# Weight sums and quarters on VectorE, TensorE's order written down from the layers' turn on, and another order of the seven products

## The chip, the cores and the metric

The kernel runs on one core of one Trainium2 chip. The metric is the device time of one execution in microseconds (us), as the median of several runs. Five engines work beside each other, each through its own instruction queue in order: TensorE (PE; its weight loads are shown as PEld), VectorE (DVE), ScalarE (ACT), GpSimd (POOL) and SyncE (SP), which here mostly issues DMA transfers.

## The reference

Two residual layers over 1024 tokens of width 1024. Each normalises its input by rows, scales and shifts it with vectors that come from a condition `c`, mixes tokens, and projects back.

```python
for layer in range(DEPTH):
    mod = jnp.einsum("bd,de->be", cond, ada_w[layer]) + ada_b[layer]
    shift, scale, gate = jnp.split(mod, 3, axis=-1)
    h = rms_norm(x, pre_gain[layer]) * (1.0 + scale[:, None, :]) + shift[:, None, :]
    if layer % N_MIXERS == 0:
        y = diff_attention(h, ...)      # 8 heads, softmax over 1024 keys
    else:
        y = retention(h, w_in, w_out)   # 4 heads, chunkwise state
    x = x + gate[:, None, :] * rms_norm(y, post_gain[layer])
...
# retention: q, k, v, g = split(h @ w_in); per chunk: scores, state, outputs
out = head_rms_norm(inner_out + cross)
y = silu(g) * out
return y @ w_out
```

## The kernel before

Every f32 matrix is split into two f16 parts, so that a product takes three matmuls for each 128x128 block of weights: high by high, high by low, low by high.

**Layer 0** (attention) ends with the output projection. `out0(t)` multiplies the rows of tile t (48 matmuls, L566), and `residual` and `row_rsqrt` turn them into the next layer's normalised rows `x`: an ACT square with a sum (L578), a DVE product (L579), three small POOL operations on 128x1 (L580, L581 and the power in `rsqrt`, L144), a DVE update `xres` (L583), an ACT square again (L295), two POOL operations (L296, L144), and a DVE scaling (L621).

**The turn.** `out0_hT(j)` takes the rows of tiles 2j and 2j+1, transposes them on PE with the identity matrix (16 transposes, L643) into the two PSUM banks `ps_sc`, lets ACT scale and shift each out of there (L645), and forms sums and differences of the four quarters (`hq`, L651 to L653; on POOL for j of 0 to 2, on DVE for j = 3), each then split into f16 parts (L660 on ACT, L661 on DVE). The list `order` says in which order tiles, transposes and projections are written, "... h0 o4 y6 h1 o5 y7 o6 h2 o7 h3"; a scheduler then sets each engine's real order.

**Layer 1** (retention) multiplies by its input weights in Strassen-Winograd form: seven products of quarter blocks in place of eight. `Columns` holds one unit of weights, 512 columns of queries and keys, of values, or of gates; there are 12 units, three for each of the four heads. `Columns.prepare` loads the quarters `B11`, `B21`, `B12`, `B22` as 128x1024 f32 tiles, forms the sums `T1` to `T4` by four additions on POOL (L779), and splits each into f16 parts (`w`, L792 on ACT, L793 on DVE). Three products are prepared ahead. `Quarters.product(n)` runs product n of `PRODUCTS` (24 matmuls at 256 columns or 12 at 512, L819) for two halves m. Products of one chain letter (`x`, `y`, `z`) accumulate in one PSUM bank; between them ACT copies the bank's state to `held` or `sg` (L827), or DVE combines it with a copy (L833). Chain `y` and later `z` of the second half sit in the single bank `ps_tr`.

The gate columns of a head run with its chunk work between the products: `scores` (L967 on PE, read out by DVE L974), `state` (L991 on PE, L999 and L1002 on DVE), `outputs` (L1014 and L1021 on PE, ACT square L295, the two POOL operations of `row_rsqrt`, DVE L1027). After span 3, `ada_gate` computes a piece of the gate vector (DVE L171 and L173, PE L245, DVE L246 and L247).

**Output products.** For each row tile t the loop at L1134 multiplies by `wo1` (L1142, 36 matmuls for heads 0 to 2 and 12 for head 3, in two column halves n). The weights are loaded by SP (L1106) and split by ACT and DVE (L1110, L1111); the rows come by transposing DMAs (L1126, L1128, L1130), which SP issues too.

Of the kernel before, what the change touches and what calls it, by code (L numbers as in the profile page):

```python
# [87 lines left out]
def trunk(ctx: ExitStack, tc: tile.TileContext, a: dict, out: bass.AP):  # L88
# [143 lines left out]
    def ada_gate(l, j):  # L232
# [11 lines left out]
        ps = tr()  # L244
        nc.tensor.matmul(ps[:, 0:256], ones, acc, start=True, stop=True)  # L245
        nc.vector.tensor_tensor(out=bias, in0=ps[:, 0:256], in1=bias, op=ALU.add)  # L246
        nc.vector.scalar_tensor_tensor(out=gps[l][:, sl], in0=bias, scalar=1.0 / SOUT, in1=gps[l][:, sl], op0=ALU.mult, op1=ALU.mult)  # L247
# [886 lines left out]
    for t in range(NT):  # L1134
        if t + 1 < NT:
            out1_yT(t + 1)
# [43 lines left out]
```

## Time and profile before

| | us |
|---|---|
| median of 3 runs (lowest to highest) | 1421.53 (1421.28 to 1422.03) |
| the profiled execution's own time | 1421.59 |
| its span, first to last instruction | 1419.7 |
| PE busy | 1301.3 (92%) |
| DVE busy | 918.2 (65%) |
| ACT busy | 665.5 (47%) |
| POOL busy | 283.5 (20%) |

The span is what the trace covers; the execution's own time holds 1.9 us more around it. Busy time is a sum over the whole span, so that an engine at 92% can still be waiting in a few places. [...] The idle time in brackets in a timeline is what the engine stood still just before an instruction, with the instruction that ended it.

### The profile page before, as it was taken

What the parts mean: (1) busy time and instruction counts of PE and PEld (TensorE: products, weight loads), DVE (VectorE), ACT (ScalarE), POOL (GpSimd) and SP (SyncE); (2) the same over time, 40 slices, a digit from 0 to 9 for tenths busy, and PEclk for the clock granted to TensorE, in tenths of its full rate; (3) what the DMA queues carried; (4) which work ended last, traced back from release to release, by engine and by line L of the source; (5) the groups of instructions that cost most, each with busy time, mean ns of one, the idle gap of its engine ahead of it and who ended that gap; (6) DMA issues with size and microseconds to landing.
All of it is one profiled execution on the core that took longest, in us unless ns stands there. A gap on an engine that the chain in (4) does not pass through costs nothing.

```text
span 1419.7 us, 21306 instructions
## 1 busy us (share of the span) xinstructions
PE 1301.3 (92%) x8285; PEld 778.7 (55%) x8285; DVE 918.2 (65%) x1722; ACT 665.5 (47%) x1262; POOL 283.5 (20%) x342
## 2 busy tenths in 40 slices
PE   4999999899999997877898999989998999979998
PEld 2445455445455444446786568755865486624443
DVE  5866987996986786765566755766585648841011
ACT  5855545553654664745353545444454535620000
POOL 2000110110111221671234122322222221100000
PEclk9999999999999999998999999999999999999999
DMA  9813564655542566423311251224221543473430
GB/s 298 251 57 76 125 136 122 137 110 126 132 98 47 141 163 107 132 89 86 83 52 60 82 150 55 67 72 132 74 75 37 153 112 119 112 177 70 101 90 30
DMA packets 249174, 153.94 MB, mean 108 GB/s; under 512 B 147576, under 2 KB 237872, under 8 KB 249072
## 3 DMA queue, kind: packets, MB, share of 16 engines
q1 hardware_dynamic: 245904, 141.29, 38.6%
q0 software_dynamic: 3168, 11.28, 2.6%
q8 instruction: 65, 1.06, 0.3%
q14 instruction: 37, 0.30, 0.1%
HBM read 102.21 MB, written 14.68 MB: 82 GB/s over the span
## 4 chain that ended last, share of the span: by engine, by line
PE 33%; DVE 9%; issue 3%; DMA 3%; ACT 3%; POOL 3%; SPq 1%; POOLq 0%; DVEq 0%; ACTq 0%
PE ps_mm L819 15%; PE ps_mm L1142 11%; PE ps_tr L819 4%; DVE w L793 2%; POOL raw L779 2%; DMA raw<-in_ada_w 2%; PE ps_av L1014 1%; DVE y L938 1%; DVE acc L173 1%; DVE sg L833 1%; DVE vr L929 1%; DMA raw<-in_ret_w_in 1%; ACT w L792 1%; PE ps_sc L991 1%; PE ps_av L1021 1%
## 5 line engine op out<-in xcount | busy, mean ns | idle before, releaser
L793 DVE SCALAR_TENSOR_TENSOR w<-raw,w 128x1024 f16<-128x1024 f32 x82 | 118.1, 1440 | 97.8 <-ACT w L792 97.8
L335 PE MATMUL ps_mm<-w,hT 128*128 128x512 f16 x768 | 175.7, 379 | 0.0
L779 POOL TENSOR_TENSOR raw<-raw,raw 128x1024 f32<-128x1024 f32 x48 | 122.4, 2549 | 207.2 <-DVE w L793 189.9
L819 PEld LDWEIGHTS <-hS 128*128 128x128 f16 x1536 | 150.0, 98 | 21.3 <-issue 1.1
L323 PE MATMUL ps_mm<-hT,w 128*128 128x512 f16 x624 | 142.2, 379 | 0.0
L819 PE MATMUL ps_mm<-w,hS 128*128 128x256 f16 x1152 | 132.1, 273 | 0.0
L515 ACT ACTIVATE sb<-sb,mx 128x128 f32<-128x128 f32 (+7 forms) x128 | 98.2, 768 | 63.5 <-DVE mx L508 62.9
L335 PEld LDWEIGHTS <-hT 128*128 128x128 f16 x768 | 74.3, 98 | 82.4
L819 PEld LDWEIGHTS <-w 128*128 128x128 f16 x744 | 75.2, 101 | 74.0 <-issue 9.3
L792 ACT ACTIVATE w<-raw 128x1024 f16<-128x1024 f32 x82 | 86.0, 1048 | 40.7 <-POOL raw L779 15.3
L1142 PE MATMUL ps_mm<-wo,yT 128*128 128x512 f16 x480 | 104.1, 379 | 0.0
L323 PEld LDWEIGHTS <-w 128*128 128x128 f16 x624 | 60.2, 98 | 67.4
L508 DVE CUSTOM_DVE_ANT_0 sb<-ps_sc,table 128x512 f32<-128x512 f32 (+3 forms) x128 | 73.5, 587 | 35.6 <-PE ps_sc L505 27.1
L579 DVE TENSOR_TENSOR po<-ps_mm,gp 128x512 f32<-128x512 f32 x16 | 11.1, 692 | 127.9 <-ACT junk L578 127.9
L566 PE MATMUL ps_mm<-w_o,yT 128*128 128x512 f16 x384 | 93.2, 387 | 0.0
L578 ACT ACTIVATE junk<-ps_mm 128x512 f16<-128x512 f32 x32 | 19.0, 593 | 147.8 <-PE ps_mm L1142 141.1
L819 PE MATMUL ps_mm<-w,hA 128*128 128x256 f16 x768 | 87.9, 273 | 0.0
L819 PEld LDWEIGHTS <-hA 128*128 128x128 f16 x768 | 74.8, 98 | 9.7
L1142 PEld LDWEIGHTS <-yT 128*128 128x128 f16 x480 | 47.0, 98 | 56.6
L173 DVE SCALAR_TENSOR_TENSOR acc<-raw,cond,acc 128x256 f32<-128x256 f32 x140 | 70.9, 517 | 7.1 <-DMA raw<-in_ada_w 5.6
L1142 PE MATMUL ps_mm<-wo,held 128*128 128x512 f16 x288 | 65.3, 388 | 10.3 <-ACT wo L1110 6.3
L819 PE MATMUL ps_mm<-hS,w 128*128 128x512 f16 (+1 forms) x312 | 62.7, 362 | 8.9 <-ACT held L827 8.9
(203 smaller groups left out, 2314.4 us busy)
## 6 DMA issues: line engine op xcount, KB each, us to landing
raw<-in_ret_w_in SPq DMA_DIRECT2D x60, 512.0 KB, 3.6
raw<-in_ada_w SPq DMA_DIRECT2D x40, 512.0 KB, 6.6
raw<-in_da_w_in SPq DMA_DIRECT2D x16, 1024.0 KB, 5.8
raw1o<-in_ret_w_out SPq DMA_DIRECT2D x16, 512.0 KB, 4.7
y_d<-y SPq DMA_DIRECT2D x6, 1024.0 KB, 4.8
x<-in_x SPq DMA_DIRECT2D x8, 512.0 KB, 7.6
raw<-in_ada_w SPq DMA_DIRECT2D x4, 1024.0 KB, 5.2
raw_o<-in_da_w_out SPq DMA_DIRECT2D x4, 1024.0 KB, 5.0
```

Of the source, the lines that this page charges most:

```text
L173: nc.vector.scalar_tensor_tensor(out=acc, in0=parts[k], scalar=cond[:, k : k + 1], in1=acc, op0=ALU.mult, op1=ALU.add)
L323: nc.tensor.matmul(ps, w[:, k, wi, lo : lo + P], hT[k][g][:, xi, :], start=(k == 0 and wi == 0 and xi == 0), stop=(k == NK - 1 and wi == 1),)
L335: nc.tensor.matmul(ps, hT[k][g][:, xi, j * P : (j + 1) * P], w[:, k, wi, :], start=(k == 0 and wi == 0 and xi == 0), stop=(k == NK - 1 and ...
L508: nc.vector.tensor_tensor_reduce(out=sb[:, c, k], in0=ps[c][:, 0:n], in1=table[:, S - L + lo : S - L + lo + n], scale=-es, scalar=(3.0e38 ...
L515: nc.scalar.activation(out=sb[:, c, 0:L], in_=sb[:, c, 0:L], func=AF.Exp, scale=-1.0, bias=mx[:, m0 + c : m0 + c + 1], accum_out=z[:, 4 * ...
L566: nc.tensor.matmul(ps, yT(yi, k), wo[k // 4][:, k % 4, wi, n * 512 : (n + 1) * 512], start=(k == 0 and yi == 0 and wi == 0), stop=(k == NK ...
L578: nc.scalar.activation(out=junk[:, 0:512], in_=src[n], func=AF.Square, accum_out=ss[:, n : n + 1])
L779: add = lambda o, x: nc.gpsimd.tensor_tensor(out=r[o], in0=r[o], in1=r[x], op=ALU.add)
L792: nc.scalar.activation(out=w[:, :, 0, :], in_=r[name], func=AF.Copy, scale=SW)
L793: nc.vector.scalar_tensor_tensor(out=w[:, :, 1, :], in0=r[name], scalar=SW, in1=w[:, :, 0, :], op0=ALU.mult, op1=ALU.subtract)
L819: nc.tensor.matmul(ps[:, pc], l, r, start=(first and i == 0 and k == 0 and wi == 0 and xi == 0), stop=(k == 3 and wi == 1), skip_group_che ...
L1142: nc.tensor.matmul(ps[n], yT1[t][2 * (k // 8) + yi][:, k % 8, :], wo1[k // 4, n][:, k % 4, wi, :], start=(k == 0 and yi == 0 and wi == 0), ...
```

## The change

- The sums of weights in `prepare` and all sums of quarters in `out0_hT` go to DVE.
- From step `o6` on, TensorE's order is the written one; the scheduler no longer orders that engine. The step `h3` leaves the list and stands inside the first unit, behind product 2 of its first half of tokens.
- The fourth of the seven products is now `("z", "S1", "T1")`; before it was the sixth. The reload of `B22` moves to the step of `T4`.
- `ada_gate` returns its second half (matmul and two DVE operations). In layer 1 its sums are written two spans earlier, and the second half stands behind the last span.
- `gated` works on one tile of 512 columns at a time in each head, where heads 0 to 2 took 2048 at once.
- The output products of tiles 0 and 1 run heads 0 to 2 of the first column half for both tiles, then of the second half, then head 3; the second half's sums sit in the bank pair `ps_av`.
- `rsqrt` takes the second addend itself, so that `residual` has two POOL operations in place of three, and scales go into the ACT square.
- Some tiles (`y`, `sg`, `vr`, `y1`) move to the other side of SBUF, and the four `kN` tiles become one.

```diff
@@ rsqrt, residual @@
+    def rsqrt(ss, eps, other=None):
+        r = small.tile([P, 2], F32, name="rs", bufs=6)
+        if other is None:
+            nc.gpsimd.tensor_scalar(out=r[:, 1:2], in0=ss, scalar1=eps, scalar2=None, op0=ALU.add)
+        else:
+            nc.gpsimd.tensor_scalar(out=r[:, 1:2], in0=ss, scalar1=other, scalar2=eps, op0=ALU.add, op1=ALU.add)
+        nc.gpsimd.tensor_tensor(out=r[:, 0:1], in0=r[:, 1:2], in1=negh[:, 0:1], op=ALU.pow)
+        return r[:, 0:1]
...
-        nc.gpsimd.tensor_tensor(out=ss[:, 0:1], in0=ss[:, 0:1], in1=ss[:, 1:2], op=ALU.add)
-        nc.gpsimd.tensor_scalar(out=ss[:, 3:4], in0=ss[:, 0:1], scalar1=1.0 / (D * SOUT**2), scalar2=NORM_EPS, op0=ALU.mult, op1=ALU.add)
-        r = rsqrt(ss[:, 3:4], 1)
+        r = rsqrt(ss[:, 0:1], NORM_EPS, ss[:, 1:2])
@@ out0_hT @@
-            eng = nc.vector if j == 3 else nc.gpsimd
             for i in range(2):
-                eng.tensor_tensor(out=t2[:, i], in0=t[:, 1], in1=t[:, 3 * i], op=ALU.subtract)
+                nc.vector.tensor_tensor(out=t2[:, i], in0=t[:, 1], in1=t[:, 3 * i], op=ALU.subtract)
...
@@ order @@
-        "o1 b5 a6 a7 b6 y4 o2 b7 f0 y5 o3 h0 o4 y6 h1 o5 y7 o6 h2 o7 h3"
+        "o1 b5 a6 a7 b6 y4 o2 b7 f0 y5 o3 h0 o4 y6 h1 o5 y7 o6 h2 o7"
     )
     for c in order.split():
+        if c == "o6":
+            ctx.enter_context(tc.manual_schedule(engines={mybir.EngineType.PE}))
@@ layer 1 @@
     PRODUCTS = (
-        ("x", "A11", "B11"), ("y", "A12", "B21"), ("x", "M2", "T2"), ("x", "N3", "T3"),
-        ("x", "A22", "T4"), ("z", "S1", "T1"), ("z", "N4", "B22"),
+        ("x", "A11", "B11"), ("y", "A12", "B21"), ("x", "M2", "T2"), ("z", "S1", "T1"),
+        ("x", "N3", "T3"), ("x", "A22", "T4"), ("z", "N4", "B22"),
     )
...
-            add = lambda o, x: nc.gpsimd.tensor_tensor(out=r[o], in0=r[o], in1=r[x], op=ALU.add)
+            add = lambda o, x: nc.vector.tensor_tensor(out=r[o], in0=r[o], in1=r[x], op=ALU.add)
...
+                            if g == 0 and (n, m) == (2, 1):
+                                out0_hT(3)
...
-                        if n == 3:
-                            ada_gate(1, h)
+                        if n == 1:
+                            st["gate"] = ada_gate(1, h)
+                        elif n == 6:
+                            st["gate"]()
@@ output products @@
+    def out1(t, n, hs):
+        if (t, n) not in pso:
+            pso[t, n] = av() if n else mm()
+        for k in [4 * h + i for h in hs for i in range(4)]:
+            for yi, wi in ((0, 0), (0, 1), (1, 0)):
+                nc.tensor.matmul(...)
...
+    for n in range(2):
+        for t in range(2):
+            out1(t, n, (0, 1, 2))
+    for t in range(NT):
+        if 2 <= t + 1 < NT:
+            out1_yT(t + 1)
+        for n in range(2):
+            out1(t, n, (3,) if t < 2 else range(RET_HEADS))
+        out1_end(t)
```

**ACT at the turn.** These are ACT's instructions before the change from the first weight copies of layer 1 on (`w<-raw`; L578 squares a projection, L295 squares the updated rows `xres`, L645 takes transposes out of `ps_sc`). `raw_6215` is the tile that becomes `T2`, the last of three sums.

```order
L792 ACTIVATE w_6217<-raw_6209 128x4x256
L578 ACTIVATE junk,ss<-ps_mm 128x512
L792 ACTIVATE w_6220<-raw_6211 128x4x256
L792 ACTIVATE w_6226<-raw_6215 128x4x256
L295 ACTIVATE junk,ss<-xres 128x1024
L792 ACTIVATE w_6229<-raw_6213 128x4x256
L578 ACTIVATE junk,ss<-ps_mm 128x512
L792 ACTIVATE w_6267<-raw_6211 128x4x256
L578 ACTIVATE junk,ss<-ps_mm 128x512
```

After the change the same stretch reads as follows; L810 is the copy, L586 and L304 the two squares, L653 the read-out, and `raw_6152` becomes `T2`.

```order
L586 ACTIVATE junk,ss<-ps_mm 128x512
L810 ACTIVATE w_6154<-raw_6146 128x4x256
L810 ACTIVATE w_6157<-raw_6148 128x4x256
L304 ACTIVATE junk,ss<-xres 128x1024
L586 ACTIVATE junk,ss<-ps_mm 128x512
L810 ACTIVATE w_6163<-raw_6152 128x4x256
L810 ACTIVATE w_6166<-raw_6146 128x4x256
L586 ACTIVATE junk,ss<-ps_mm 128x512
L653 ACTIVATE hq<-ps_sc,mod_0_1426 128x2x128
L810 ACTIVATE w_6203<-raw_6150 128x4x256
```

The square of `xres` (L295, now L304) has moved ahead of the copy of `T2`, and one more copy stands inside the read-outs.

**POOL and DVE in the gate columns of head 0.** Before the change POOL has the four sums of the next unit ahead of the two operations of one span's `row_rsqrt`:

```order
L779 TENSOR_TENSOR raw_7341<-raw_7341,raw_7443 128x1024
L779 TENSOR_TENSOR raw_7443<-raw_7443,raw_7562 128x1024
L779 TENSOR_TENSOR raw_7562<-raw_7562,raw_7341 128x1024
L779 TENSOR_TENSOR raw_7441<-raw_7441,raw_7562 128x1024
L296 TENSOR_SCALAR ss<-ss,dec 128x1
L144 TENSOR_TENSOR rs<-ss,negh 128x1
```

and DVE, at the same place, has the span's scaling (L1027), the gate vector, and then the read-out of the scores (L974):

```order
L793 SCALAR_TENSOR_TENSOR w_7660<-raw_7441,w_7660 128x4x256
L1002 SCALAR_TENSOR_TENSOR sh<-st_7197,sh 128x512 x2
L1027 TENSOR_SCALAR y_6725<-ps_av,rs 128x512
L246 TENSOR_TENSOR gbias<-ps_tr,gbias 128x256
L247 SCALAR_TENSOR_TENSOR gp<-gbias,gp 128x256
L974 TENSOR_TENSOR a_7599<-ps_sc,dec 128x128
```

After the change DVE holds three sums (L798) around that read-out (L1002; L1055 is the scaling, L811 the split of a weight):

```order
L811 SCALAR_TENSOR_TENSOR w_7554<-raw_7351,w_7554 128x4x256
L1030 SCALAR_TENSOR_TENSOR sh<-st_7191,sh 128x512 x2
L1055 TENSOR_SCALAR y_6690<-ps_av,rs 128x512
L798 TENSOR_TENSOR raw_7351<-raw_7351,raw_7454 128x1024
L798 TENSOR_TENSOR raw_7454<-raw_7454,raw_7552 128x1024
L1002 TENSOR_TENSOR a_7491<-ps_sc,dec 128x128
L798 TENSOR_TENSOR raw_7552<-raw_7552,raw_7351 128x1024
L1004 TENSOR_TENSOR aT<-a_7491,aT 128x128
```

POOL has no sum left there, and the gate vector is no longer between the scaling and the read-out.

**SP at the output products.** Before the change these DMAs stand between the last gate columns and the first output products; L1126 to L1130 are the transposes, `raw1o` the weights:

```order
L1106 DMA raw1o<-in_ret_w_out 128x2x512
L1130 DMA_TRANSPOSE held<-y_10904 128x4x128
L1126 DMA_TRANSPOSE yT<-y_d 128x8x128
L1130 DMA_TRANSPOSE held<-y_10904 128x4x128
L1126 DMA_TRANSPOSE yT<-y_d 128x8x128
L1128 DMA_TRANSPOSE yT<-y_d 128x4x128 x2
L1130 DMA_TRANSPOSE yT<-y_10904 128x4x128 x4
L1106 DMA raw1o<-in_ret_w_out 128x2x512 x5
```

After the change (L1136 loads weights, L1156 to L1160 transpose):

```order
L1136 DMA raw1o<-in_ret_w_out 128x2x512 x2
L1160 DMA_TRANSPOSE held<-y_10979 128x4x128
L1160 DMA_TRANSPOSE yT<-y_10979 128x4x128
L1160 DMA_TRANSPOSE held<-y_10979 128x4x128
L1156 DMA_TRANSPOSE yT<-y_d 128x8x128 x2
L1158 DMA_TRANSPOSE yT<-y_d 128x4x128 x2
L1160 DMA_TRANSPOSE yT<-y_10979 128x4x128 x3
L1136 DMA raw1o<-in_ret_w_out 128x2x512 x8
```

Eight loads of weights, those of the second column half, now stand behind the transposes; before it was five.

## Rows read from the trace of the kernel before

**Rows 1.** Busy time of the engines in four stages (h0 and h1, turn, layer 1, output products)

```profile
568.00:606.00 38.00, 32.55 (x179) 16.38 (x178) 28.54 (x33) 27.33 (x57) 25.38 (x36) 1.00 0.52 137
606.00:690.00 84.00, 62.21 (x409) 43.43 (x407) 51.76 (x64) 39.59 (x80) 37.32 (x34) 0.86 0.26 77
690.00:1234.00 544.00, 519.71 (x3852) 372.11 (x3850) 351.07 (x462) 260.77 (x391) 137.29 (x107) 0.98 0.32 90
1234.00:1262.00 28.00, 17.69 (x72) 7.22 (x70) 18.09 (x24) 11.89 (x17) 1.23 (x2) 0.88 0.71 178
```

**Rows 2.** The same view, sums over stretches at half clock: turn, heads, output products

```profile
sum 23.90, PE 14.63 PEld 9.91 DVE 18.59 ACT 15.12 POOL 6.26; mean PE 4.88 PEld 3.30 DVE 6.20 ACT 5.04 POOL 2.09
...
sum 17.06, PE 14.50 PEld 5.43 DVE 13.62 ACT 8.64 POOL 1.47; mean PE 4.83 PEld 1.81 DVE 4.54 ACT 2.88 POOL 0.49
...
sum 6.83, PE 4.66 PEld 1.53 DVE 4.90 ACT 4.59 POOL 0.00; mean PE 4.66 PEld 1.53 DVE 4.90 ACT 4.59 POOL 0.00
```

**Rows 3.** Timeline of the turn at 605 us: start, us, in brackets idle before

```profile
605.56 11.14 POOL L779 TENSOR_TENSOR raw<-raw,raw 128x1024 f32<-128x1024 f32 x4
606.28 3.37 DVE L583 SCALAR_TENSOR_TENSOR xres<-x,rs,xres 128x1024 f32<-128x1024 f32 x1
...
614.30 1.06 ACT L792 ACTIVATE w<-raw 128x1024 f16<-128x1024 f32 x1 [9.41 <-POOL raw L779]
...
619.32 0.90 PE L643 MATMUL ps_sc<-ident,x 128*128 128x128 f32 x3 [6.72 <-DVE x L621]
619.52 0.92 POOL L580 TENSOR_TENSOR ss<-ss 128x1 f32<-128x1 f32 x1 [1.05 <-ACT junk L578]
```

**Rows 4.** Timeline of the turn at 645 us

```profile
642.50 2.75 ACT L645 ACTIVATE hq<-ps_sc,mod 128x256 f32<-128x256 f32 x5 [2.13 <-PE ps_sc L643]
...
652.20 1.01 PE L819 MATMUL ps_mm<-hS,w 128*128 128x256 f16 x4 [3.44 <-ACT held L827]
```

**Rows 5.** Timeline of the turn at 675 us

```profile
678.74 2.56 DVE L853 SCALAR_TENSOR_TENSOR qT<-held,qT 128x256 f16<-128x256 f32 x1
681.05 1.06 ACT L792 ACTIVATE w<-raw 128x1024 f16<-128x1024 f32 x1 [5.93 <-POOL raw L779]
...
682.43 1.44 PE L819 MATMUL ps_mm<-hS,w 128*128 128x256 f16 x6 [5.42 <-ACT held L827]
```

**Rows 6.** Groups by line and form: busy us, mean ns, idle before

```profile
L779 POOL TENSOR_TENSOR raw<-raw,raw 128x1024 f32<-128x1024 f32 x48 | 122.4, 2549 | 207.2 <-DVE w L793 189.9 <-DMA raw<-in_ret_w_in 14.8
...
L793 DVE SCALAR_TENSOR_TENSOR w<-raw,w 128x1024 f16<-128x1024 f32 x82 | 118.1, 1440 | 97.8 <-ACT w L792 97.8
...
L1033 DVE TENSOR_TENSOR sg<-y,sg 128x2048 f32<-128x2048 f32 x6 | 13.7, 2287 | 4.0 <-ACT sg L1032 4.0
...
L660 ACT ACTIVATE hS<-hq 128x512 f16<-128x512 f32 x16 | 9.9, 624 | 8.6 <-POOL hq L653 7.4 <-POOL hq L651 0.7 <-DVE hq L653 0.4
...
L1033 DVE TENSOR_TENSOR sg<-y,sg 128x512 f32<-128x512 f32 x8 | 5.3, 686 | 0.0
```

**Rows 7.** Timeline of the first head's gate columns at 775 us

```profile
772.50 7.72 POOL L779 TENSOR_TENSOR raw<-raw,raw 128x1024 f32<-128x1024 f32 x3 [4.56 <-DMA raw<-in_ret_w_in]
...
774.98 2.78 PE L819 MATMUL ps_mm<-w,hA 128*128 128x256 f16 x24
...
781.14 0.75 DVE L1027 TENSOR_SCALAR y<-ps_av,rs 128x512 f32<-128x512 f32 x1 [7.96 <-POOL rs L144]
...
782.94 1.03 PE L991 MATMUL ps_sc<-y,kN 128*128 128x512 f16 x3 [4.53 <-DVE a L974]
```

**Rows 8.** Timeline of the first output products

```profile
1234.32 1.89 PE L1142 MATMUL ps_mm<-wo,held 128*128 128x512 f16 x8
...
1245.76 3.83 PE L1142 MATMUL ps_mm<-wo,held 128*128 128x512 f16 x17 [3.30 <-DVE wo L1111]
...
1250.02 7.51 SPq L1106 DMA_DIRECT2D raw1o<-in_ret_w_out  x5
...
1255.93 0.59 PE L1142 MATMUL ps_mm<-wo,held 128*128 128x512 f16 x1 [6.34 <-ACT wo L1110]
```

More of the change, by code (lines that the diff above doesn't have):

```diff
@@ L243, in ada_gate, with rest @@
             acc = ada_sum(*(raw_block(a["ada_w"][l, i * 512 : (i + 1) * 512, 2 * D + j * 256 : 2 * D + (j + 1) * 256]) for i in range(2)))
[L244 to L247, printed above, removed]
+        def rest():
+            ps = tr()
+            nc.tensor.matmul(ps[:, 0:256], ones, acc, start=True, stop=True)
+            nc.vector.tensor_tensor(out=bias, in0=ps[:, 0:256], in1=bias, op=ALU.add)
+            nc.vector.scalar_tensor_tensor(out=gps[l][:, sl], in0=bias, scalar=1.0 / SOUT, in1=gps[l][:, sl], op0=ALU.mult, op1=ALU.mult)
+        return rest
     def new_w():
@@ L294, in row_rsqrt @@
         ss = small.tile([P, 4], F32, name="ss", bufs=6)
-        nc.scalar.activation(out=junk[:, 0 : src.shape[-1]], in_=src, func=AF.Square, accum_out=ss[:, 0:1])
-        nc.gpsimd.tensor_scalar(out=ss[:, 3:4], in0=ss[:, 0:1], scalar1=scale / n, scalar2=eps, op0=ALU.mult, op1=ALU.add)
-        return rsqrt(ss[:, 3:4], 1)
+        nc.scalar.activation(out=junk[:, 0 : src.shape[-1]], in_=src, func=AF.Square, scale=math.sqrt(scale / n), accum_out=ss[:, 0:1])
+        return rsqrt(ss[:, 0:1], eps)
     x_v = a["x"].rearrange("b (t p) d -> p (b t) d", p=P)
@@ L676, in piece @@
             if c == "g":
-                ada_gate(0, h - 1)
+                ada_gate(0, h - 1)()
             else:
@@ L748, in trunk, with ret2 @@
     ret = l1.enter_context(tc.tile_pool(name="ret", bufs=1, reuse_waits="tile"))
+    right = []
+    def ret2():
+        if not right:
+            l0y.close()
+            right.append(l1.enter_context(tc.tile_pool(name="ret2", bufs=1, side="right", reuse_waits="tile")))
+        return right[0]
     held = lambda dtype=F32, shape=(P, 512): ret.tile(list(shape), dtype, name="held", tag="held", bufs=5)
@@ L1055, in step @@
                         outputs(*SPANS[n])
-                        if n == 3:
-                            ada_gate(1, h)
+                        if n == 1:
+                            st["gate"] = ada_gate(1, h)
+                        elif n == 6:
+                            st["gate"]()
                     if n == 6 and u == 1:
                         for uu in range(2):
-                            for ts in [slice(i, i + 1) for i in range(4)] if h == RET_HEADS - 1 else [slice(0, 4)]:
-                                gated(uu, ts)
+                            for i in range(4):
+                                gated(uu, slice(i, i + 1))
                 steps1.append((c_g, n, step))
@@ L1131, in out1_yT, with out1_end @@
         yT1[t] = ps_
[L1133 to L1145 removed]
+    pso = {}
+    def out1(t, n, hs):
[3 more added lines that the diff above has]
+            for yi, wi in ((0, 0), (0, 1), (1, 0)):
+                nc.tensor.matmul(
+                    pso[t, n], yT1[t][2 * (k // 8) + yi][:, k % 8, :], wo1[k // 4, n][:, k % 4, wi, :],
+                    start=(k == 0 and yi == 0 and wi == 0), stop=(k == 15 and yi == 1),
+                )
+    def out1_end(t):
         xt = ws1.tile([P, D], F32, name="xr1", tag="w1")
@@ L1148, in trunk @@
         po = ws1.tile([P, D], F32, name="po", tag="w1")
-        hs, add = residual(ps, po, gps[1], xt, xt)
+        hs, add = residual([pso[t, n] for n in range(2)], po, gps[1], xt, xt)
         for sl in hs if t == NT - 1 else [slice(0, D)]:
@@ L1152, in trunk @@
             nc.sync.dma_start(out=out_v[:, t, sl], in_=xt[:, sl])
+    for t in range(2):
+        out1_yT(t)
+    for n in range(2):
+        for t in range(2):
+            out1(t, n, (0, 1, 2))
[5 more added lines that the diff above has]
+        out1_end(t)
 _INS = [
```

56 lines of the change are left out of this document (24 added, 32 removed).

## The prediction

> **What bounds the kernel now.** I read the busy shares first: TensorE (PE) is busy for 92% of the span, so no edit can win much by making work smaller on another engine, and PE's own work is the same before and after. What can be won is PE's idle time and PE's time at half clock. So I cut the part that the change touches into four stages [rows 1] and subtracted PE's busy time from each. Idle are 38.00 - 32.55 = 5.5 us where h0 and h1 run, 84.00 - 62.21 = 21.8 us at the turn, 544.00 - 519.71 = 24.3 us in layer 1, and 28.00 - 17.69 = 10.3 us at the start of the output products: 61.9 us.
>
> Then the granted clock. It is 0.86 at the turn and 0.88 at the output products [rows 1]. [...]
>
> Last I looked at what ends each wait. At the turn POOL sums weights for 11.14 us in a row; ACT, in order, stands 9.41 us before a copy of one of those sums; and the square of the updated rows is queued behind that copy, so that PE waits 6.72 us for the rows x [rows 3]. Further on PE waits 3.44 us for a copy into `held`, behind ACT's read-out of h3's transposes [rows 4], and 5.42 us for another one, behind an ACT that waited 5.93 us for a POOL sum [rows 5]. In the gate columns of a head POOL sums for 7.72 us, its two small operations of `row_rsqrt` come behind, DVE waits 7.96 us for them with the scores' read-out queued behind that, and PE waits 4.53 us for the read-out [rows 7]. One cause runs through three of these four: long POOL sums ahead of something short in an in-order queue.
>
> **The change part by part.** *The price of a sum on DVE.* The trace has no such DVE instruction at 128x1024. The same kind of operation took 686 ns at 512 columns and 2287 ns at 2048 [rows 6]; a line through both gives 1.22 us at 1024, against 2.55 us on POOL. The 48 sums then add 48 x 1.22 = 58.6 us to DVE, and take 122.4 us from POOL. In layer 1's window some 40 of them add 49 us to DVE's 351: 400 of about 515 us, or 78%. The quarters' sums (24 on POOL before, by the same line about 0.42 us each on DVE) add 10 us. Against this, splits of weights took 1.44 us in the mean [rows 6], and a 128x256 combination 2.56 us beside POOL's sums [rows 5]; if those come free, the 82 splits give back up to 82 x (1.44 - 1.22) = 18 us.
>
> *h0 and h1.* ACT stood 7.4 us before POOL's quarters [rows 6]; with these on DVE I count 3 of the 5.5 us (bounds 0 and 5.5).
>
> *The turn, idle time.* First wait (6.72): three sums now take 3 x 1.22 = 3.7 us instead of most of 11.14, and the order of ACT has the square of the rows ahead of the copy of T2. But PE's order is now a written one, and the sixteen transposes of h2 stand in one piece with two banks to go into; ACT empties a bank in 2 x 0.55 us (2.75 us for five read-outs [rows 4]), with a weight copy of 1.06 us [rows 3] now and then ahead of it. I leave 3 us. Middle: h3 now stands behind six blocks of 12 matmuls, so its rows are ready, but its read-outs are still ahead of a copy to `held`; with some of the 6.2 us of small waits that the three named ones leave of 21.8, I leave 3 us. Last wait (5.42): its sum is no longer on POOL; I leave 1 us. So 7 of 21.8 us stay: a gain of 14.8 (bounds: 5.42 alone, or all 21.8). *The turn, clock.* With waits that short I let 5.3 of the 7.3 us come back (bounds 0 and 7.3).
>
> *Heads.* The 4.53 us wait comes once in each of the first three heads, 13.6 us of the 24.3; the rest are short waits for DVE read-outs. After the change POOL has nothing ahead of `row_rsqrt`, and DVE has two sums ahead of the read-out of the scores: 2 x 1.22 = 2.4 us. PE has a product of 24 matmuls, 2.78 us [rows 7], to do meanwhile, so that the wait is nearly covered. Without that cover it would be 2.4 us in each of three heads. I leave 5 of 24.3: a gain of 19.3 (bounds 13.6 and 24.3), and let the clock's 7.2 come back. *New waits in layer 1.* Forty sums of 1.22 us now stand on the engine that also combines the products. A read-out that finds one running waits 0.6 us in the mean: 40 x 0.6 = 24 us, of which PE's queue of matmuls should cover most. I take a loss of 4 us (bounds 0 and 12, half of it).
>
> *Output products.* Before, the first product began at 1234.32 and the last wait ended at 1255.93, 21.6 us later [rows 8], for weights whose loads were issued behind ten transposes on SP. Those loads are behind ten transposes still, now eight of them, not five. What changes is PE's order: two row tiles of the first column half come first, 2 x 36 matmuls at 3.83/17 = 0.225 us, or 16.2 us. So 21.6 - 16.2 = 5.4 us of waiting stay of 10.3: a gain of 4.9, and the clock there as it was (bounds: 0, and 10.3 + 2.3 = 12.6).
>
> *Counted at nothing.* One POOL operation less of 0.92 us [rows 3] in each `residual` counts only where PE waits for the rows; that is inside the turn's terms, and at the end of the kernel it is under a microsecond. `gated` in pieces adds to DVE 4 x 0.686 - 2.287 = 0.46 us for each 2048-wide operation [rows 6], six of them on the line shown, beside products of PE; without that cover it is some 3 us. The gate vector's order is in the heads' term; the tiles' new places change no duration that I can point to.
>
> *Sum.* 3 + 14.8 + 5.3 + 19.3 + 7.2 - 4 + 4.9 = 50.5 us. The profiled execution's own time was 1421.59 us (span 1419.7), level with the median of 1421.53. So 1421.6 - 50.5 = 1371 us.
>
> [...] A DVE update of 128x1024 that ran beside POOL's sums took 3.37 us [rows 3], and the combination 2.56 us [rows 5], far over the line above (1.22 and 0.42): beside POOL's sums DVE stands still for part of the time. The same could hold the other way round, DVE's sums stopping POOL's small operations; one took 0.92 us for 128x1 [rows 3]. [...]
>
> **The rivals.** (a) *PE's written order waits.* At the turn a scheduler chose PE's order before; a fixed one stands at every late read-out, sixteen transposes in two banks above all. Then the turn's gains fall to the last wait: 5.4 in place of 20.1 us, and the time is 1371 + 14.7 = 1386. For it speaks ACT's load there (39.59 of 84 us [rows 1], most of it around the transposes); against it, that the weight sums which blocked ACT are shorter by half. (b) *DVE's sums hold up POOL.* Each of the two operations of a row's rsqrt waits for one sum, 2.4 us a chain; with four chains at the turn and two in each of three heads on PE's path, 10 x 2.4 = 24 us go, and the time is 1395. Against it: most chains have no sum beside them. (c) *The output products' waits stay or grow,* since three more loads are behind the transposes; at 7.51 us for five issues [rows 8], 3 x 1.5 = 4.5 us more, so the gain of 4.9 becomes about 0: 1376. (d) *DVE becomes the bound: slower.* POOL was idle for most of layer 1 and DVE was not; 58.6 + 10 = 68.6 us move to the busier engine. [...] Against it: DVE's 78%, and up to 18 us that come back from undisturbed splits. (e) *The change does nothing,* since the waits for POOL were only the last of several that end together: 1421. [...]
>
> **How the numbers follow.** My forecast of 1371 has a chance of 0.55, with a range of its own from 1358 to 1382; (a) 0.15, (b) 0.08, (c) 0.09, (d) 0.06, (e) 0.03, (f) 0.04. The range of 8 in 10 leaves out (d), (e), half of (f) and the outer part of (b): 1355 to 1395. A measurement of this kernel can tell about 0.2%, or 2.8 us, from no change. Faster by more: all but (d) and (e), some of which fall on that side too, 0.92; within it 0.03; slower 0.05.
>
> **What would show it.** *Right:* no POOL instruction of 128x1024 is left; DVE's sums take about 1.2 us and splits of weights about 1.25; PE's idle time is near 10 us at the turn and in layer 1 each; the waits of 4.5 us in the heads are gone, with a granted clock of 1.00 there; DVE's busy time in layer 1 is about 400 us. *Wrong:* sums of 2 us or more on DVE; waits of PE at the transposes of h2 or h3 that end with ACT's read-out (a); POOL's 128x1 operations of 2 us or more (b); a wait over 6 us before the second column half of the output products (c); waits of PE for DVE's read-outs spread over all of layer 1 (d).

## The result, and the profile after

The changed kernel takes 1381.42 us in the median (1377.45 to 1382.68, 4 runs), the kernel before 1421.4. The ratio is 0.9714 (95% interval 0.9694 to 0.9735): 40 us or 2.9% faster. Forecast were 1371 us, in a range of 1355 to 1395. Three of the four stages gained what was forecast to within 2 us; the turn gave some 11 us less.

The four stages of [rows 1] in the changed kernel, between the same events (busy time and instruction count of PE, PEld, DVE, ACT and POOL, then granted clock as a share of PE's full one, DMA share, GB/s):

```profile
569.45:605.00 35.55, 32.87 (x179) 16.15 (x178) 28.06 (x49) 27.36 (x58) 9.30 (x17) 1.00 0.57 148
605.00:679.24 74.24, 60.50 (x409) 42.90 (x407) 50.74 (x80) 38.28 (x79) 9.20 (x16) 0.86 0.22 76
679.24:1201.10 521.86, 512.94 (x3852) 369.86 (x3850) 381.71 (x538) 264.52 (x430) 44.70 (x67) 1.00 0.33 93
1201.10:1229.10 28.00, 23.66 (x105) 10.20 (x105) 17.12 (x21) 11.04 (x15) 0.86 (x2) 1.00 0.79 219
```

PE's idle time is the length less PE's busy time: 2.7 us where h0 and h1 run (5.5 before), 13.7 at the turn (21.8), 8.9 in layer 1 (24.3), 4.3 in 28 us of the output products (10.3). The clock is whole again (1.00) in the last two stages. At the turn it is 0.86, as before. The two stretches at half clock (0.50) there, as windows:

```profile
613.80:627.46 13.66, 8.03 (x24) 4.08 (x25) 12.69 (x22) 10.79 (x22) 3.20 (x5) 0.50 0.46 154
647.93:654.76 6.83, 4.88 (x22) 3.51 (x23) 5.98 (x14) 5.62 (x12) 0.00 (x0) 0.50 0.17 54
```

PE was busy in them for 12.91 us. Twelve matmuls in the second one (at 651.47, clock 0.50) took 2.77 us, 24 of the same form behind it (at 655.70, clock 1.00) 2.78; the rows ahead of them are PE's waits at h3's transposes (L651):

```profile
645.12 0.66 PE L651 MATMUL ps_sc<-ident,x 128*128 128x128 f32 x4 [1.18 <-ACT hq L653]
646.67 0.66 PE L651 MATMUL ps_sc<-ident,x 128*128 128x128 f32 x4 [0.89 <-ACT hq L653]
648.22 1.11 PE L651 MATMUL ps_sc<-ident,x 128*128 128x128 f32 x4 [0.89 <-ACT hq L653]
650.99 0.69 PE L651 MATMUL ps_sc<-ident,x 128*128 128x128 f32 x2 [1.66 <-ACT hq L653]
651.47 2.77 PE L837 MATMUL ps_mm<-hS,w 128*128 128x256 f16 x12
...
655.70 2.78 PE L837 MATMUL ps_mm<-hS,w 128*128 128x256 f16 x24
```

So half of that busy time, 6.5 us, was lost; 2 us had been forecast. The timeline of the first stretch, at h2's transposes (L651), answers to [rows 3]:

```profile
609.72 3.73 DVE L798 TENSOR_TENSOR raw<-raw,raw 128x1024 f32<-128x1024 f32 x3
...
612.23 2.00 ACT L810 ACTIVATE w<-raw 128x1024 f16<-128x1024 f32 x2 [5.12 <-DVE raw L798]
...
614.71 0.55 ACT L653 ACTIVATE hq<-ps_sc,mod 128x256 f32<-128x256 f32 x1
615.15 1.05 ACT L810 ACTIVATE w<-raw 128x1024 f16<-128x1024 f32 x1
...
615.31 1.12 PE L651 MATMUL ps_sc<-ident,x 128*128 128x128 f32 x4 [3.61 <-ACT hq L653]
...
617.17 1.11 PE L651 MATMUL ps_sc<-ident,x 128*128 128x128 f32 x4 [0.74 <-ACT hq L653]
...
618.97 1.11 PE L651 MATMUL ps_sc<-ident,x 128*128 128x128 f32 x4 [0.69 <-ACT hq L653]
619.33 1.05 ACT L304 ACTIVATE junk<-xres 128x1024 f16<-128x1024 f32 x1
...
620.67 1.14 ACT L667 ACTIVATE hS<-hq 128x512 f16<-128x512 f32 x2
...
621.71 1.01 ACT L653 ACTIVATE hq<-ps_sc,mod 128x256 f32<-128x256 f32 x2
...
622.77 0.69 PE L651 MATMUL ps_sc<-ident,x 128*128 128x128 f32 x2 [2.69 <-ACT hq L653]
```

The old pattern is still there with another engine in it: ACT stands 5.12 us before the copy of a sum (now DVE's), and what is queued behind, now the read-out of the first transposes, comes late. Then the sixteen transposes crawl from bank to bank while ACT squares rows (L304) and splits quarters (L667) between its read-outs.

The groups that price the sums, by line and form (busy us, mean ns of one, idle before):

```profile
L811 DVE SCALAR_TENSOR_TENSOR w<-raw,w 128x1024 f16<-128x1024 f32 x82 | 99.9, 1220 | 56.8 <-ACT w L810 56.8
...
L798 DVE TENSOR_TENSOR raw<-raw,raw 128x1024 f32<-128x1024 f32 x48 | 58.7, 1222 | 1.1
```

A sum takes 1222 ns (forecast 1.22 us), 58.7 us in all (58.6). The splits fell from 1440 ns [rows 6] to 1220, which gives back 18.2 us (up to 18 forecast). DVE's busy time in layer 1 is 382 us, where 400 had been counted without that.

### The profile page after: what moved, and what is told of

The parts are those of the page before. It is cut to its first block, busy times and chain, and to the rows that moved or that the text cites. A ratio compares the mean times of both kernels' runs of the same rounds, so it can differ in the third digit from the quotient of the medians.

```text
span 1379.8 us, 21360 instructions
## 1 busy us (share of the span) xinstructions
PE 1291.8 (94%) x8285; PEld 775.2 (56%) x8285; DVE 948.4 (69%) x1830; ACT 669.3 (49%) x1298; POOL 146.7 (11%) x254
## 4 chain that ended last, share of the span: by engine, by line
PE 42%; DVE 5%; ACT 5%; DMA 2%; POOL 1%; issue 1%; SPq 0%; POOLq 0%; DVEq 0%; ACTq 0%
PE ps_mm L837 20%; PE ps_av L1170 6%; PE ps_mm L1170 5%; PE ps_tr L837 5%; PE ps_sc L1019 2%; PE ps_av L1042 1%; PE ps_av L1049 1%; DMA raw1o<-in_ret_w_out 1%; PE ps_mm L574 1%; DMA raw<-in_ada_w 1%; ACT junk L304 1%; ACT sg L1060 1%; POOL rs L149 1%; POOL rs L146 1%; DVE w L811 1%
## 5 line engine op out<-in xcount | busy, mean ns | idle before, releaser
L811 DVE SCALAR_TENSOR_TENSOR w<-raw,w 128x1024 f16<-128x1024 f32 x82 | 99.9, 1220 | 56.8 <-ACT w L810 56.8
L810 ACT ACTIVATE w<-raw 128x1024 f16<-128x1024 f32 x82 | 85.8, 1049 | 53.9 <-issue 33.7
L1170 PEld LDWEIGHTS <-yT 128*128 128x128 f16 x480 | 46.9, 98 | 56.7
L178 DVE SCALAR_TENSOR_TENSOR acc<-raw,cond,acc 128x256 f32<-128x256 f32 x140 | 65.6, 480 | 10.7 <-DMA raw<-in_ada_w 9.2
L534 ACT ACTIVATE sb<-sb 128x896 f16<-128x896 f32 (+6 forms) x64 | 43.3, 678 | 55.4 <-DVE sb L531 55.3
L546 PEld LDWEIGHTS <-dT 128*128 128x128 f16 x864 | 53.7, 99 | 28.5 <-DMA dT<-sb 20.1
L512 PE MATMUL ps_sc<-ks,qs 128*128 128x512 f16 (+3 forms) x192 | 62.1, 330 | 6.9 <-DVE mx L516 6.7
L513 PE MATMUL ps_sc<-kl,qs 128*128 128x512 f16 (+3 forms) x192 | 62.0, 329 | 0.0
L574 PEld LDWEIGHTS <-yT 128*128 128x128 f16 x384 | 38.1, 100 | 41.8 <-issue 3.8
```

Source lines behind the costliest of these rows:

```text
L178: nc.vector.scalar_tensor_tensor(out=acc, in0=parts[k], scalar=cond[:, k : k + 1], in1=acc, op0=ALU.mult, op1=ALU.add)
L512: nc.tensor.matmul(ps[c][:, 0:n], qs[:, c, q], ks[:, c, k], start=True, stop=False)
L513: nc.tensor.matmul(ps[c][:, 0:n], qs[:, c, q], kl[c][:, k], start=False, stop=True)
L574: nc.tensor.matmul(ps, yT(yi, k), wo[k // 4][:, k % 4, wi, n * 512 : (n + 1) * 512], start=(k == 0 and yi == 0 and wi == 0), stop=(k == NK ...
L810: nc.scalar.activation(out=w[:, :, 0, :], in_=r[name], func=AF.Copy, scale=SW)
L811: nc.vector.scalar_tensor_tensor(out=w[:, :, 1, :], in0=r[name], scalar=SW, in1=w[:, :, 0, :], op0=ALU.mult, op1=ALU.subtract)
```

## The experiments

To compare the kernels' profiles I cut each one at the same instructions of PE: the first matmul of layer 0's output projection, the first product of the third unit (end of the turn), the first output product, and the end of the last one. The turn of this table is therefore longer than the window of the same name above: it holds the whole output projection and the first two units. The first column of times is the median, the others are lengths of these stretches in us, in brackets PE's idle time in it. Each ratio is to runs of the kernel before that were taken beside that kernel. The end of the kernel is 6 to 7 us in all.

| kernel | median | ratio to before (interval) | layer 0 | turn | heads | output |
|---|---|---|---|---|---|---|
| before | 1421.4 | 1 | 495.3 | 226.8 (38.0) | 512.3 (24.1) | 178.9 (10.3) |
| changed | 1381.4 | 0.9714 (0.9694-0.9735) | 497.8 | 213.2 (26.3) | 490.4 (8.9) | 172.2 (5.1) |
| e1 | 1394.7 | 0.9821 (0.9804-0.9837) | 495.5 | 223.0 (33.0) | 496.3 (13.5) | 171.4 (4.4) |
| e2 | 1378.2 | 0.9702 (0.9689-0.9716) | 496.2 | 212.0 (26.8) | 482.8 (2.6) | 178.2 (8.0) |
| e3 | 1365.9 | 0.9621 (0.9606-0.9637) | 495.0 | 199.5 (17.5) | 491.0 (9.3) | 171.7 (4.5) |
| e4 | 1374.4 | 0.9678 (0.9664-0.9692) | 496.8 | 213.9 (25.9) | 490.1 (9.0) | 167.6 (0.0) |
| e5 | 1356.6 | 0.9549 (0.9534-0.9564) | 497.8 | 200.7 (17.2) | 482.8 (2.5) | 169.6 (3.1) |
| e6 | 1394.5 | 0.9824 (0.9806-0.9843) | 496.1 | 223.5 (35.6) | 496.7 (14.5) | 167.6 (0.0) |
| e7 | 1411.7 | 0.9939 (0.9924-0.9955) | 497.4 | 224.5 (35.9) | 511.9 (25.5) | 168.7 (2.3) |
| e8 | 1387.3 | 0.9771 (0.9757-0.9785) | 496.3 | 211.4 (26.0) | 490.7 (9.1) | 179.6 (10.7) |
| e9 | 1377.0 | 0.9686 (0.9668-0.9705) | 497.0 | 210.1 (24.3) | 490.2 (8.6) | 172.5 (5.4) |
| e10 | 1359.8 | 0.9571 (0.9553-0.9590) | 496.3 | 204.5 (20.9) | 482.3 (2.0) | 169.9 (3.4) |
| e11 | 1387.5 | 0.9763 (0.9748-0.9777) | 496.2 | 221.1 (31.9) | 490.7 (9.1) | 171.3 (4.2) |
| e12 | 1390.0 | 0.9779 (0.9758-0.9799) | 496.0 | 226.2 (35.6) | 490.1 (8.8) | 171.7 (3.6) |

**The sums alone.** e1 takes the sums out of the change, e2 puts only the sums into the kernel before.

```diff
-            add = lambda o, x: nc.vector.tensor_tensor(out=r[o], in0=r[o], in1=r[x], op=ALU.add)
+            add = lambda o, x: nc.gpsimd.tensor_tensor(out=r[o], in0=r[o], in1=r[x], op=ALU.add)
```

(e1; e2 is the reverse, in the kernel before.)

> The changed kernel with one edit: the four sums of weights in prepare back on POOL. Theory (long POOL sums ahead of short instructions in in-order queues were the loss): the waits of about 4.5 us in the gate columns of the first three heads come back and ACT waits for POOL sums at the turn again, so 20 to 30 us of the 40 are lost: 1401 to 1412 us. Rival (the heads gained by the other order of the products and the gate vector's new place, the sums' engine matters little): under 1390 us, and no wait over 3 us in the heads.

> The kernel before with one edit: the four sums of weights in prepare on DVE, everything else as it was. Theory: this edit alone brings most of the gain, 20 to 30 us: 1391 to 1401 us, with the heads' waits of 4.5 us gone. Rival (it needs the new order of products and gate vector, since DVE's queue now holds the sums ahead of the scores' read-out): 1412 us or more, and the heads still wait, now for DVE.

e2 is 42 us faster than before, more than was expected: one word in one line gives all that the whole change gives, and the heads are shorter than in the changed kernel (482.8 against 490.4 us). But e1 lost only some 15 us (0.0107 of 1421), less than expected, and its heads show no wait over 3 us: 496.3 us, near the changed kernel's and far from the 512.3 before. So something else in the change cures the same waits, and the two don't add. What the sums on POOL do to DVE is plain in e1, by line and form:

```profile
L811 DVE SCALAR_TENSOR_TENSOR w<-raw,w 128x1024 f16<-128x1024 f32 x82 | 126.9, 1552 | 84.5 <-ACT w L810 84.5
L798 POOL TENSOR_TENSOR raw<-raw,raw 128x1024 f32<-128x1024 f32 x48 | 123.4, 2571 | 190.0 <-DVE w L811 184.0 <-issue 3.6
```

The same split takes 1552 ns with POOL's sums beside it and 1220 without.

**What the other cure is.** e6 is e1 with the products in the order of before (the edit of e4, below), e7 has the gate vector back behind span 3 too; e12 moves in e7 only the gate's sums.

```diff
@@ e7 to e12 @@
-                        if n == 3:
-                            ada_gate(1, h)()
+                        if n == 1:
+                            st["gate"] = ada_gate(1, h)
+                        elif n == 3:
+                            st["gate"]()
```

> The changed kernel with the sums of weights on POOL and the products in the order of before; the gate vector and the written order stay new. It asks what kept the heads free of the waits of 4.5 us when the sums went back to POOL. Theory (the new order of products did, by moving sums away from spans): the waits come back, heads of 147 us and more, 1400 us or more in all. Rival (the gate vector's new place did, since it stood between the scaling and the scores' read-out on DVE): heads stay at about 144.5 us and the time at 1388 to 1396 us.

> The kernel of the run before this one with the gate vector also back after span 3: only the sums' engine, the products' and the gate's order are as before, TensorE's order is written. Theory (products' order or gate vector cured the heads): waits of 4 us and more in three heads, heads of 149 to 151 us, 1405 us or more. Rival (the written order of TensorE cured them): heads of about 145 us, under 1398 us.

> The slowest of the runs so far (weight sums on POOL, products and gate vector as before, written order) with one edit: the gate vector's sums two spans earlier, its matmul and its two last DVE operations still after span 3. Theory (the gate's two blocks sit in the same buffers as the weights' quarters, so that the last quarter's load comes late and three POOL sums run just ahead of the scores' rsqrt; where the DVE operations stand matters little): the waits of 4.3 to 5.2 us go, heads of 144 to 145 us, 1392 to 1398 us. Rival (the two DVE operations between the scaling and the read-out made the wait): heads stay at 150 us, 1408 to 1413 us.

My theory of e6 fell (the products' order is not the cure: heads of 496.7 us); with the gate vector back the waits return (e7: 511.9 us), though the order of TensorE is a written one. e12 then shows which part of the gate vector it is: not its two operations in DVE's queue, which stay where they were, but its sums. e7, first head, around the wait of PE, in the timeline:

```profile
753.01 6.10 SPq L773 DMA_DIRECT2D raw<-in_ada_w  x2
...
766.18 2.65 DVE L178 SCALAR_TENSOR_TENSOR acc<-raw,cond,acc 128x256 f32<-128x256 f32 x2
...
768.86 0.37 SPq L773 DMA_DIRECT2D raw<-in_ret_w_in  x1
...
772.56 7.53 POOL L798 TENSOR_TENSOR raw<-raw,raw 128x1024 f32<-128x1024 f32 x3 [4.53 <-DMA raw<-in_ret_w_in]
...
780.06 0.29 POOL L146 TENSOR_SCALAR rs<-ss,dec 128x1 f32<-128x1 f32 x1
...
782.84 1.44 PE L1020 MATMUL ps_sc<-y,kN 128*128 128x512 f16 x3 [4.34 <-DVE a L1003]
```

The gate's blocks (`in_ada_w`) are loaded into the same four buffers as the weights' quarters. The last quarter is loaded at 768.86, right behind the gate's last sum (766.18 + 2.65 = 768.83); POOL had stood 4.53 us for it, and so it does its three sums in one piece just when the scores' `row_rsqrt` is due. In e12 the quarters come in time and the same sums leave room for the small operations between them:

```profile
741.95 13.72 SPq L773 DMA_DIRECT2D raw<-in_ret_w_in  x4
...
762.43 2.73 POOL L798 TENSOR_TENSOR raw<-raw,raw 128x1024 f32<-128x1024 f32 x1 [5.74 <-DVE w L812]
765.15 0.72 POOL L146 TENSOR_SCALAR rs<-ss,dec 128x1 f32<-128x1 f32 x1
...
766.49 4.80 POOL L798 TENSOR_TENSOR raw<-raw,raw 128x1024 f32<-128x1024 f32 x2
...
772.50 2.68 POOL L798 TENSOR_TENSOR raw<-raw,raw 128x1024 f32<-128x1024 f32 x1 [1.22 <-issue]
775.16 0.73 POOL L146 TENSOR_SCALAR rs<-ss,dec 128x1 f32<-128x1 f32 x1
```

Its heads take 490.1 us, as long as those of the changed kernel, with every sum of weights on POOL.

**The written order of TensorE.** e3 gives the order back to the scheduler; e9 keeps the written one, but splits h2's transposes; e11 puts h3 back into the list.

```diff
@@ e3 @@
-            ctx.enter_context(tc.manual_schedule(engines={mybir.EngineType.PE}))
+            pass
@@ e9 @@
-        ps = outproj(yTs[t], wts["o"])
+        part = out0_hT(2) if t == 7 else iter(())
+        ps = outproj(yTs[t], wts["o"], lambda: next(part, None))
...
@@ e11 @@
-        "o1 b5 a6 a7 b6 y4 o2 b7 f0 y5 o3 h0 o4 y6 h1 o5 y7 o6 h2 o7"
+        "o1 b5 a6 a7 b6 y4 o2 b7 f0 y5 o3 h0 o4 y6 h1 o5 y7 o6 h2 o7 h3"
...
-                            if g == 0 and (n, m) == (2, 1):
-                                out0_hT(3)
```

In e9 `out0_hT` yields after each four transposes, and `outproj` of tile 7 calls it after each twelve matmuls.

> The changed kernel with one edit: TensorE's order from o6 on is set by the scheduler again, not written. Theory (the written order costs something at the turn, where sixteen transposes of h2 stand in one row behind ACT): 1372 to 1379 us, the idle time at the transposes of h2 falls from 7.7 us to under 4. Rival (the written order is what shortened the turn and keeps the heads free of waits): 1388 us or more.

> The changed kernel, written order kept, but the sixteen transposes of h2 written in four groups of four, each followed by twelve matmuls of o7, where before they stood in one piece ahead of o7. Theory (the written order lost its 14 us at h2, where PE stood behind ACT's read-outs and then ran at half clock): idle time at h2's transposes falls from 7.7 us to under 3, the half-clock stretch of 13.7 us there shrinks, 1369 to 1376 us. Rival (it lost them elsewhere, at h3 and in the order of the first unit): 1378 to 1383 us.

> The changed kernel with h3 back at the end of the list, ahead of the first unit's products, in the written order. Theory (inside the first unit its rows are ready and products cover its read-outs): 3 to 8 us slower, 1384 to 1389 us, with a wait of 5 us or more for the rows of tile 7. Rival (its read-outs cost PE as much in either place): within 3 us of 1381.

e3 is 13 us faster than the changed kernel (0.9714 - 0.9621 = 0.0093 of 1421), all of it at the turn (199.5 against 213.2). The transposes by line in the changed kernel:

```profile
L651 PE MATMUL ps_sc<-ident,x 128*128 128x128 f32 x64 | 14.2, 334 | 15.0 <-ACT hq L653 13.0 <-DVE x L629 1.9
```

in e3, and under it the window of its turn:

```profile
L651 PE MATMUL ps_sc<-ident,x 128*128 128x128 f32 x64 | 13.6, 305 | 6.7 <-DVE x L629 3.7 <-ACT hq L653 2.7
...
603.40:672.60 69.20, 64.50 (x498) 48.34 (x496) 53.54 (x89) 40.41 (x86) 9.96 (x15) 1.00 0.37 109
```

and in e9:

```profile
L656 PE MATMUL ps_sc<-ident,x 128*128 128x128 f32 x64 | 12.8, 295 | 12.4 <-ACT hq L658 10.2 <-DVE x L634 2.0
```

In e3, which is faster than its theory had it, the idle time before transposes is 8.3 us shorter in sum (15.0 - 6.7) and the clock at the turn is 1.00, which is worth the 6.5 us lost in the changed kernel: 14.8, a little over the 13 measured. The wait does not go because ACT is faster: in e3 too ACT stands 5.13 us before the copy (first row below, of its timeline). The scheduler writes the transposes two or four at a time, with matmuls between them, so that PE has work while ACT reads out:

```profile
610.43 2.00 ACT L810 ACTIVATE w<-raw 128x1024 f16<-128x1024 f32 x2 [5.13 <-DVE raw L798]
...
613.51 0.44 PE L651 MATMUL ps_sc<-ident,x 128*128 128x128 f32 x2 [1.68 <-ACT hq L653]
...
614.25 1.24 PE L574 MATMUL ps_mm<-w_o,yT 128*128 128x512 f16 x5
...
615.37 0.44 PE L651 MATMUL ps_sc<-ident,x 128*128 128x128 f32 x2
```

e9 does this by hand and for h2 alone. It gained 4 us, at the edge of what its interval and the changed kernel's can tell, and by its time it stands between both expectations. PE still waits four times at h2 (1.97, 0.98, 0.82 and 1.01 us, 4.8 in all, where under 3 was expected); the half-clock stretch at h2 did shrink, from 13.7 to 3.4 us, but the one at h3 stayed. So by these times h2 in one piece is about a third of the loss, and the rest lies elsewhere in the written order; how much of it around h3 and how much in finer pieces of h2 was not tried. e11 shows that under the written order the new place of h3 is right: at the end of the list PE waits 6.10 us for the rows of tile 7, and the turn is 8 us longer.

**Products, quarters, output loop, and three parts undone.** e4 and e8 are edits of the changed kernel, e5 has e3's, e4's and the old gate vector together, and e10 is an edit of e5.

```diff
@@ e4 (and the numbers of products in product and queries_keys, and the reload of B22) @@
-        ("x", "A11", "B11"), ("y", "A12", "B21"), ("x", "M2", "T2"), ("z", "S1", "T1"),
-        ("x", "N3", "T3"), ("x", "A22", "T4"), ("z", "N4", "B22"),
+        ("x", "A11", "B11"), ("y", "A12", "B21"), ("x", "M2", "T2"), ("x", "N3", "T3"),
+        ("x", "A22", "T4"), ("z", "S1", "T1"), ("z", "N4", "B22"),
@@ e8 @@
+        for hs in ((0, 1, 2), (3,)):
+            for n in range(2):
+                out1(t, n, hs)
+        out1_end(t)
@@ e5, beside e3 and e4 @@
-                        if n == 1:
-                            st["gate"] = ada_gate(1, h)
-                        elif n == 6:
-                            st["gate"]()
+                        if n == 3:
+                            ada_gate(1, h)()
@@ e10, in e5 @@
+            eng = nc.vector if j == 3 else nc.gpsimd
             for i in range(2):
-                nc.vector.tensor_tensor(out=t2[:, i], in0=t[:, 1], in1=t[:, 3 * i], op=ALU.subtract)
+                eng.tensor_tensor(out=t2[:, i], in0=t[:, 1], in1=t[:, 3 * i], op=ALU.subtract)
```

> The changed kernel with the seven products in the order of before (S1 by T1 sixth, the reload of B22 at its step); the gate vector stays where the change put it. Theory (the order of the products moves no wait that PE feels): 1378 to 1385 us. Rival (the earlier product gives the preparation of T3 and T4 time, and fewer combinations wait): 1390 us or more, with waits of PE ahead of products in all twelve units.

> The changed kernel with the output products row tile by row tile, as before. Theory (the new loop brought what the output stage gained, since 16 us of work stand before the first weights of the second column half): 5 to 8 us slower, 1386 to 1389 us, with a wait of 4 to 6 us before the second half's first product. Rival (the loads' arrival decides, the loop moves the wait only): within 3 us of 1381.

> The kernel of the three undone parts with the sums of quarters of h0 to h2 back on POOL. Theory (ACT waits for POOL's quarters and PE for ACT at h0 to h2): 3 to 7 us slower, 1359 to 1364 us. Rival (h0 to h2 are covered by the output projection and POOL, free of weight sums, is soon enough): 1355 to 1358 us.

> The changed kernel with three parts undone at once: TensorE's order from the scheduler, the products in the order of before, the gate vector computed whole after span 3. The sums and quarters on DVE, the output loop and the rest stay. Theory (the written order costs about 14 us at the turn, the products' order about 6 in the heads and output, and the two add): 1355 to 1362 us, heads of about 142 us each. Rival (the old products' order paid only under the written order): 1364 to 1369 us, no better than the scheduler's order alone.

e4 is faster than either theory had it, by 5 us against the changed kernel (the intervals are just apart); the heads are the same (490.1), and the gain stands in the output products, where PE doesn't wait at all. The first weights of the second column half are there in time: SP has five loads behind the transposes, as in the first row below (e4), where the changed kernel has eight, as in the second block:

```profile
1213.45 8.01 SPq L1137 DMA_DIRECT2D raw1o<-in_ret_w_out  x5
...
1218.01 7.93 PE L1171 MATMUL ps_av<-wo,held 128*128 128x512 f16 x36
```

```profile
1208.42 1.45 PE L1170 MATMUL ps_mm<-wo,held 128*128 128x512 f16 x6 [1.45 <-DVE wo L1141]
...
1213.71 10.94 SPq L1136 DMA_DIRECT2D raw1o<-in_ret_w_out  x8
...
1220.30 5.47 PE L1170 MATMUL ps_av<-wo,held 128*128 128x512 f16 x24 [0.88 <-DVE wo L1141]
```

That the products' order alone decides this is not shown: six kernels with the old order and the new loop took 167.6 to 171.7 us here, five with the new order 171.3 to 172.5.

e8, with the old loop, is 8 us slower than the changed kernel by the ratios (0.0057 of 1421) and 7.4 in the stage, as its theory had it; PE waits 7.58 us in one place ahead of the second half, where 4 to 6 had been expected. e10 moves the quarters' sums of e5 back to POOL and loses 3.2 us, though the intervals overlap; the profiles agree (the turn is 3.7 us longer).

e5 undoes three parts of the change and is the best kernel of the study: 1356.6 us, 4.5% faster than before (0.9549) and 23 us by the ratios faster than the changed kernel. The turn is 12.5 us shorter than in the changed kernel, much as in e3, the output products are 2.6 us shorter, and the heads, with the gate vector back behind span 3 and the sums on DVE, fell to 482.8 us, as in e2.

What the gate vector's new place costs the heads of the changed kernel stands in its trace. The gate's matmul (L252) is written behind the last product there and goes into the same bank, `ps_tr`; once in each head PE waits ahead of it until DVE has read that product out (L846). The first head:

```profile
784.76 0.68 DVE L846 TENSOR_TENSOR sg<-ps_tr,sg 128x512 f32<-128x512 f32 x1
...
785.50 0.70 PE L252 MATMUL ps_tr<-acc,ones 128*128 128x256 f32 x2 [0.85 <-DVE sg L846]
```

The four waits are 0.85, 1.20, 1.21 and 0.90 us, 4.2 of the 8.9 us that PE is idle in the heads. In e2, e5, e7, e10 and e12, where this matmul stands behind span 3, there is none over 0.3 us. e6 and e12 differ in its place alone: the heads take 496.7 and 490.1 us, and by the ratios e12 is 6 us faster (0.9824 - 0.9779 of 1421). So of the gate vector's two moves the early sums help, by some 22 us beside sums on POOL (e7 to e12), and the late second half costs. What the early sums alone do beside sums on DVE was not tried, and neither were `gated` in pieces, the shorter `rsqrt` and the tiles' places by themselves.

## Why the prediction held, and where it failed

The time lies in the range, but nearer to rival (a)'s 1386 us than to 1371: the total held and one of its terms did not.

*h0 and h1:* forecast 3 us, measured 5.5 - 2.7 = 2.8 in the windows. Right. With the quarters of h0 to h2 back on POOL the kernel is 3.2 us slower (e10 against e5, with intervals that overlap).

*Heads and new waits:* forecast 19.3 - 4 of idle time and 7.2 of clock, 22.5 in all. The windows show 24.3 - 8.9 = 15.4 and a clock of 1.00, and the stage is 544.00 - 521.86 = 22.1 us shorter. The size was right, and so was the mechanism, sums on POOL ahead of `row_rsqrt`: before and e2 differ in the sums' engine alone, and the heads take 512.3 and 482.8 us. It was not whole: I read the run of sums as given, and passed over what stood in the same row, POOL's wait of 4.56 us for a load [rows 7]. That late load is the other half of the cause, and either cure removes the waits alone (e2, e12); the change has both. For the gate vector's order I had nothing of its own, only "in the heads' term": its early sums would have done this alone (e12), and its late second half costs waits that I hadn't counted. So there is luck in the size. The 8.9 us that stay are the 5 + 4 of the forecast, but 4.2 of them are the gate's matmul, while the forty sums on DVE, for which the 4 stood, leave e2 with 2.6 us of idle time in its heads in all.

*Output products:* forecast a gain of 4.9 us with 5.4 us of waits left; measured 6.8 (178.9 - 172.2) with 5.1 left, the rest being the clock, which I had left as it was. e8 shows that the loop does it.

*The turn* is where it failed: forecast 14.8 us of idle time and 5.3 of clock, measured 21.8 - 13.7 = 8.1 and 7.3 - 6.5 = 0.8. That is 11 us too many, more than the whole difference of 10 between forecast and time; the output products gave 2 back, and layer 0 took 2.5. The forecast's clock figures, 7.3 us here, 7.2 in the heads and 2.3 at the output products, are half of PE's busy time in the stretches of [rows 2]; that half of it is lost there rests on the changed kernel's matmuls above (12 in 2.77 us at 0.50, 24 in 2.78 at 1.00). No run shows the 5.3 of 7.3 that I let come back: with the written order it is the 0.8, and in e3 the clock at the turn is 1.00. The step was "I leave 3 us" at h2's transposes, where PE waits 3.61, 0.74, 0.69 and 2.69 us, 7.7 in all, together with "with waits that short" for the clock. At h3's transposes 4.6 us stayed (the 3 there were for all small waits too), and 1.4 of the last wait, for which 1 was left. I had counted what ACT needs to empty the banks and had the right mechanism as rival (a), but argued against it that the sums which block ACT are shorter by half. They are, and ACT's wait before their copy fell from 9.41 to 5.12 us, but ACT reaches that copy early, and what is queued behind it still comes late. Rival (a) came true at some 11 of its 14.7 us, with the sign that was named for it, waits at the transposes that end with ACT's read-out; e3 shows that it was the written order that cost this.

*Layer 0*, which I left out, is 2.5 us longer in the profile of the changed kernel. 1.7 us of it is a stretch of 3.4 us at half clock near 182 us, with PE busy throughout:

```profile
180.31:183.72 3.41, 3.41 (x15) 1.49 (x13) 2.35 (x12) 2.85 (x12) 0.00 (x0) 0.50 0.94 262
```

Twelve of these kernels have the same code there (the changed one, e1, and e3 to e12). Three show this stretch, the changed one, e5 and e7, and theirs are the longest times for layer 0 (497.4 to 497.8 us, the others 495.0 to 497.0). So the same code runs with it and without it; what brings it, and what makes the rest of the 2.5 us, stays open.

*DVE beside POOL:* the splits took 1440 ns in the mean with the sums on POOL before, 1552 in e1, and 1220 with the sums on DVE. The pair before and e2 is the clean one, since only the sums' engine differs: the splits went from 1440 to 1227 ns. In the other direction POOL's first operation after a span's square went from 395 to 506 ns in the mean, by line and form before and in e2:

```profile
L296 POOL TENSOR_SCALAR ss<-ss,dec 128x1 f32<-128x1 f32 x24 | 9.5, 395 | 149.3 <-ACT junk L295 142.5 <-DVE sg L1033 6.8
```

```profile
L296 POOL TENSOR_SCALAR ss<-ss,dec 128x1 f32<-128x1 f32 x24 | 12.1, 506 | 167.9 <-ACT junk L295 138.1 <-DVE sh L1002 15.7 <-DVE gbias L246 7.4
```

That is 0.1 us where rival (b) had 1.2, a whole sum ahead of each small operation, which no run shows. The longest of them in the changed kernel took 1.68 us (L146), under the 2 us named as (b)'s sign. The longest split before took 3.36 us, 2.1 more than 1.22, and the shortest POOL sum 2.34.

*DVE as the bound* (d) didn't come: 382 of 522 us in layer 1.

## What to carry to other kernels

When several edits of one change aim at the same wait, run each alone: here moving the sums gave the whole gain, and the edits that came with it gave back as much as they brought, one of them by a wait of its own: the gate's matmul, put behind the last product, waited 0.85 to 1.21 us in each head for the bank that this product leaves. A wait that ends with a slow engine has two questions, why the engine is slow and why it started late; read the idle time in front of the slow instruction too. Before writing an engine's order down, look at what it does between the pieces of work that another engine must pick up: with h2's transposes in one piece behind two banks PE stood 15.0 us ahead of transposes in sum, with two or four at a time between matmuls 6.7 (e3).
